# Gathering the first expert pair's tokens with the one-hot matrix as the loaded operand, and moving the first iteration's small products

## The chip, the cores and the metric

The kernel runs on one core of a Trainium2 chip. The metric is the device time of one execution in microseconds (us); lower is better. Engines are named as in the profile: PE is TensorE's matmul stream, PEld its weight loads, DVE is VectorE, ACT is ScalarE, POOL is GpSimd, SP is the engine whose queue issues the weight transfers.

## The reference, cut to what matters

One layer of a hybrid decoder: a token mixer (not touched here), LayerNorm, and then a mixture of 32 experts, of which each of the 512 tokens takes two.

```python
def _hier_moe(x, wg, bg, we, be, w1, w3, w2):
    ...
    eid = (grp[:, None] * EXPERTS_PER_GROUP + top_i).reshape(-1)      # 2 experts of each token
    ...
    xs = xpad[row_tok].reshape(n_blk, MOE_BLOCK, D)                   # the tokens of each expert
    def expert_block(args):
        xb, e = args
        h = jax.nn.silu(xb @ w1[e]) * (xb @ w3[e])
        return h @ w2[e]
    ...
    out = jnp.zeros((N + 1, D), f32).at[row_tok].add(ys * row_w[:, None])

x = _layer_norm(ALPHA * x + h, ln1_g[l], ln1_b[l])      # before the experts
x = _layer_norm(ALPHA * x + h, ln2_g[l], ln2_b[l])      # after them
```

Per expert `w1` and `w3` are 1024x512 and `w2` is 512x1024, in float32: 2 MB each.

## The kernel before

All experts are worked through in 16 pairs, `for i in range(16)`. Each expert has 64 slots, so a pair fills the 128 partitions; tokens beyond 64 for an expert go through a loop at the end (`overflow`). An iteration does, on PE: the first weights' products (`ps_a` or `ps_o <- wu,xe`, W1 then W3, each 8 contraction steps for each of the two experts, which use one half of the array's columns each), transposes of `h`, the second weights' products (W2, `ps_r` and `ps_u <- wu,hT`), and the scatter (`scatter`, `ps_w <- yh,ST` and `yl,ST`), which brings the slots' rows back to the tokens and is added into `x1` by DVE (lines 1537 to 1542). `xe` holds the pair's tokens transposed: 8 pieces of 128 features by 128 slots, feature index `8p + k`.

**Where `xe` comes from.** For pairs 1 to 15 the token rows are fetched by an indirect DMA into a tile `xg` (`gather_rows`, lines 1432 to 1441, issued by POOL, of tag `xg` with two buffers), and `turn` (lines 1515 to 1522) makes 8 PE transposes of it, in two PSUM banks, which `evacuate` copies to SBUF with LayerNorm's scale and shift, alternately on ACT and DVE. Pair 0 can't wait for a DMA: its tokens are gathered by PE. `places` (line 1383) makes a one-hot matrix `G` on DVE (128 tokens by 64 slots for each expert and each of the four token tiles `t`) from the slot numbers `posm`, which `place(t)` makes from a few small products. `gather_first(t)`, lines 1399 to 1402, then makes, for each of 8 feature groups k, one product with `x1[:, t, k::8]` as the loaded operand (128x128) and `G` as the moving one (128 columns), so that the result is already transposed. Eight pieces accumulate over the four token tiles in two PSUM banks (`w` and `o`). The last token tile's slots are known last, and two throw-away products (`NWARM`) stand in front of its gather.

**The rest of iteration 0.** Besides its own products, iteration 0 has work that the others don't: `residual(0)` and `residual(1)` (lines 1552 to 1558) scale `x1` by LayerNorm's gain and shift, spread over the partitions by 8 small products each (`row`, 16 rows of the array, `ps_w <- gb,csm`) and taken in by 8 DVE operations each; `lists` (transposes of `posm`, and counts per expert), `pair(0)` to `pair(3)` (`slot_sums`, 4 small products each, then weights and token indices), `slot_places` (the scatter's matrix `ST`) and `overflow_lists` (lines 1486 to 1506, some 20 short DVE operations, whose total `toti` is later read into a register by every engine).

**PSUM.** Small results go through tag `w`, three banks used in turn, so a product waits until the bank's former content has been read.

**Weights.** They stream through a ring of ten 2 MB buffers (`wu`), 96 units in all, issued by SP in program order. `prefetch_into(w)` reuses the buffers of W1 and W3 in quarters as soon as PE has read them (line 1111); `prefetch(2)` at the end of an iteration takes the next two buffers (line 1107), which are those of the pair's W2. The order of instructions on each engine is made by a scheduler; `tc.issue_after` fixes some of it.

Of the kernel before, what the change touches and what calls it, by code (L numbers as in the profile page):

```python
# [9 lines left out]
F32 = mybir.dt.float32  # L10
# [10 lines left out]
D = 1024  # L21
NT = S // 128
KD = D // 128
# [131 lines left out]
def trunk_kernel(ctx, tc, I, cst, out, dbg_outs=None, stop=None):  # L155
# [35 lines left out]
    def bank(tag="w"):  # L191
        return ps.tile([128, 512], F32, name="ps_" + tag, tag=tag, bufs={"w": 3, "a": 2}.get(tag, 1))
# [1201 lines left out]

    places(0, range(NT - 1))
    pk = [bank(b) for b in "wo"]
    pk = [pk[k // 4][:, 128 * (k % 4):128 * (k % 4) + 128] for k in range(KD)]

    def gather_first(t):
        for k in range(KD):  # L1400
            pe.matmul(pk[k], x1[:, t, k::KD], G_[0][:, t, 0:2].rearrange("p e s -> p (e s)").bitcast(F32),
                      start=k % 4 == 0 and t == 0, stop=k % 4 == 3 and t == NT - 1, skip_group_check=True)

    iv = place(NT - 1)
    with tc.issue_after(mm.ins):
# [10 lines left out]
    def evacuate(xe, k, p):  # L1416

        if k % 2:
            return V_.tensor_scalar(xe[:, k], p, gq[:, 0, k:k + 1], gq[:, 1, k:k + 1], op0=ALU.mult, op1=ALU.add)
        else:  # L1420
            return nc.scalar.activation(xe[:, k], p, AF.Identity, scale=gq[:, 0, k:k + 1], bias=gq[:, 1, k:k + 1])

    def xtile():
        return me.tile([128, KD, 128], F32, name="xe", tag="xe", bufs=3)
# [27 lines left out]
    def pair(i):  # L1452

        p = slot_sums(i, 0, 6)
        wv = me.tile([128, 2], F32, name="wv", tag="wv", bufs=5)
        for a in range(2):
            hp = slice(64 * a, 64 * a + 64)
            V_.tensor_copy(wv[hp, 1:2], p[hp, 2 * a + 1:2 * a + 2])
            V_.tensor_add(wv[hp, 0:1], p[hp, 2 * a:2 * a + 1], wv[hp, 1:2])
        wvs[i] = wv[:, 0:1]  # L1460
        if i > 1:
            xgs[i] = gather_rows(p[:, 4:5], 128)

    xes = {0: xtile()}
    ia = [evacuate(xes[0], k, pk[k]) for k in range(KD)][-2]
    wvs, xgs = {}, {}
    xgs[1] = gather_rows(slot_sums(1, 4, 6)[:, 0:1], 128)
    with tc.issue_after(ia.ins), tc.issue_after(iv.ins):
# [17 lines left out]
    def overflow_lists():  # L1486
        ext, one32, ends, off = (sm(n, 32) for n in ("ext", "one32", "ends", "off"))
        V_.tensor_scalar(ext, cnt, 64.0, None, op0=ALU.is_gt)
        for b in range(2, 8):
            V_.scalar_tensor_tensor(ext, cnt, 64.0 * b, ext, op0=ALU.is_gt, op1=ALU.add)  # L1490
        V_.memset(one32, 1.0)
        V_.tensor_tensor_scan(ends, one32, ext, 0.0, op0=ALU.mult, op1=ALU.add)
        toti = sm("toti", 1, dt=I32)
        V_.tensor_copy(toti, ends[:, 31:32])

        V_.tensor_sub(off, ends, ext)
        V_.tensor_scalar(off, off, -1.0, 64.0, op0=ALU.add, op1=ALU.mult)
        qo = mle
        V_.tensor_add(qo, pos, off[:, None, :].to_broadcast([128, NT, 32]))
        V_.tensor_scalar(qo, qo, 1.0, None, op0=ALU.add)  # L1500
        V_.scalar_tensor_tensor(qo, pos, 64.0, qo, op0=ALU.is_ge, op1=ALU.mult)
        qp = sm("qp", 2, NT)
        for n, o in ((0, o1), (1, o2)):
            V_.tensor_mul(wse, qo, o)
            V_.tensor_reduce(qp[:, n], wse, axis=AX.X, op=ALU.add)
        return ends, toti, qp
# [3 lines left out]
    def bk(tag):  # L1510
        t = banks[tag].pop(0)
        banks[tag].append(t)
        return bank(t)

    def turn(xg, xe, n=128):

        for h in range(2):
            p = bk("w")
            for k in range(4):
                pe.transpose(p[:, 128 * k:128 * k + n], xg[0:n, 4 * h + k::KD], ident[:n, :n])  # L1520
            for k in range(4):
                evacuate(xe, 4 * h + k, p[:, 128 * k:128 * k + n])


    HALVES = [slice(0, 512), slice(512, 1024)]
# [26 lines left out]
    def residual(n):  # L1552

        g, b = row(0, n), row(1, n)
        for t in range(NT):
            xs = x1[:, t, 512 * n:512 * n + 512]
            V_.scalar_tensor_tensor(xs, xs, ALPHA, g, op0=ALU.mult, op1=ALU.mult)
            V_.scalar_tensor_tensor(xs, b, ALPHA, xs, op0=ALU.mult, op1=ALU.add)
# [76 lines left out]
    def slot_places(es):  # L1635
        p = bk("w")
        for a in range(2):
            pe.matmul(p[64 * a:64 * a + 64], idb[0:32, es[a]:es[a] + 1].to_broadcast([32, 64]), posT[0:32], start=True, stop=True)
        ST = mh.tile([128, S], F32R, name="ST", tag="ST")
        V_.tensor_scalar(ST, p, C("slot")[:, 0:1], None, op0=ALU.is_equal)  # L1640
        return ST
# [4 lines left out]
    for i in range(16):  # L1646
        es = (2 * i, 2 * i + 1)
        xe = xes.pop(i)
        end = i == 15
        hs = []  # L1650
        for n in range(2):
            w = [units.pop((n, e)) for e in es]
            p = bk("h")
            for k in range(KD):
                for a in range(2):
                    wk = zt["half"][:, k - 4] if i + n + a == 0 and k > 3 else w[a][:, k]
                    m3 = pe.matmul(p[64 * a:64 * a + 64], xe[:, k, 64 * a:64 * a + 64], wk, start=k == 0, stop=k == KD - 1)
            hs.append(p)
            if end and not n:
                scatter(1)  # L1660
                wv, ST = wvs.pop(i), slot_places(es)
            if i > PAIRS:
                prefetch_pair() if todo else None
            elif i > FINE:
                prefetch(2)
            else:
                prefetch_into(w)
        if not i:
            hst.close()
            mh = ctx.enter_context(tc.tile_pool(name="mh", bufs=1))  # L1670
        h = mh.tile([128, 4, 128], F32, name="h", tag="h")
        nc.scalar.activation(h, fmajor(hs[0]), AF.Silu)
        V_.tensor_mul(h, h, fmajor(hs[1]))  # L1673
        if i and not end:
            with tc.issue_after(m3.ins):
                scatter(1, None, range(SC))
        elif not i:
            residual(0)
            lists()
            pair(0)  # L1680
            pair(1)
            wv, ST = wvs.pop(i), slot_places(es)
        p = bk("w")
        for f in range(4):
            pe.transpose(p[:, 128 * f:128 * f + 128], h[:, f], ident)
        hT = mh.tile([128, 4, 128], F32, name="hT", tag="h")
        nc.scalar.copy(hT, p.rearrange("p (f s) -> p f s", f=4))  # L1687
        if i and not end:
            scatter(1, None, range(SC, NT))
            wv, ST = wvs.pop(i), slot_places(es)  # L1690
        if not i:
            over = overflow_lists()
            residual(1)
        if i < 15:
            xes[i + 1] = xtile()
            turn(xgs.pop(i + 1), xes[i + 1])
        if i % 2 == 0 and i < 14:
            places(2 * i + 4, range(NT))
            pair(i + 2)
            pair(i + 3)  # L1700
        w = [units.pop((2, e)) for e in es]
        cols = PARTS if end else HALVES
        for n, cs in enumerate(cols):
            last = n == len(cols) - 1
            m = cs.stop - cs.start
            p = bk("y")[:, 0:m]
            with after(mm if n else None):
                for f in range(4):
                    for a in range(2):
                        mm = pe.matmul(p[64 * a:64 * a + 64], hT[:, f, 64 * a:64 * a + 64], w[a][:, f, cs], start=f == 0, stop=f == 3)  # L1710
            if last and end:
                overflow(*over)
            elif n and not end:
                scatter(0)
            yh = mh.tile([128, 512], F32R, name="yh", tag="yh")
            yl = mh.tile([128, 512], F32R, name="yl", tag="yl")
            nc.scalar.activation(yh[:, 0:m], p, AF.Identity, scale=wv)  # L1717
            if last and end:

                nc.scalar.activation(warm2, yh[:, 0:1].bitcast(F32), AF.Sqrt, scale=0.0, bias=epsln[:, 0:1])  # L1720
            V_.scalar_tensor_tensor(yl[:, 0:m], p, wv, yh[:, 0:m].bitcast(F32), op0=ALU.mult, op1=ALU.subtract)  # L1721
            if end and not last:
                scatter(n, add_sum, cols=PARTS)
        if i > PAIRS:
            prefetch_pair() if todo else None
        else:
            prefetch(2)
        if i == 14:

            lnq = unit([128, 2, D])  # L1730
            for n, v in enumerate(("ln2_g", "ln2_b")):
                nc.sync.dma_start(lnq[:, n], I[v][0:1].to_broadcast([128, D]))
# [64 lines left out]
```

## Time and profile before

| | before |
|---|---|
| median of 3 runs (lowest to highest) | 1120.78 us (1116.54 to 1124.68) |
| the profiled execution's own time | 1121.27 us |
| its span, first to last instruction | 1119.4 us |
| mean granted TensorE clock | 0.968 of full speed |
| PE busy | 1065.9 us, 95% |
| DVE busy | 537.7 us, 48% |
| ACT busy | 337.4 us, 30% |
| POOL busy | 267.2 us, 24% |
| HBM over the span | 237 GB/s |

The expert part begins near 598 us of the span, so the busy shares above are averages over the mixer and the experts. PE's busy time counts records whose ends are modelled: a PE that is busy all the time may still be slowed, by the clock or by its weight loads. In an f32 product two records belong to one matmul.

### The profile page before, as it was taken

How to read it: one execution, taken by the hardware profiler on the slowest of the kernel's cores; microseconds unless marked ns; L12 is line 12 of the kernel's file. 1: busy time of each engine (PE TensorE's matmuls, PEld its weight loads, DVE VectorE, ACT ScalarE, POOL GpSimd, SP SyncE). 2: the span in 40 equal slices, each digit the busy share in tenths (PEclk: the TensorE clock that was granted, in tenths of full speed). 3: DMA queues.
4: the chain of work that ended last, by engine and by line, in shares of the span. 5: the costliest groups of instructions: out<-in, count | busy, mean ns of one | idle time of the engine just before them, and what ended most of it. 6: DMA issues, size and time to landing. Idle time of an engine off the chain costs nothing. (4 is left out here: it accounts for less than half of the span.)

```text
span 1119.4 us, 16299 instructions
## 1 busy us (share of the span) xinstructions
PE 1065.9 (95%) x6172; PEld 652.7 (58%) x6172; DVE 537.7 (48%) x1382; ACT 337.4 (30%) x635; POOL 267.2 (24%) x273
## 2 busy tenths in 40 slices
PE   7999998999999999998999999999999999999992
PEld 5777766767767677786899533434343434343331
DVE  3673377468747743404555643434343434333226
ACT  4443434263463344543322211111111111111103
POOL 4541353354336245432100010101010101010003
PEclk9999898999999899999999899999999999999996
DMA  8652212302212311379847769999999999999971
GB/s 232 189 135 85 62 34 49 85 29 63 57 30 52 85 40 44 110 255 330 262 158 282 273 245 416 416 414 413 412 413 416 414 415 419 428 421 405 405 275 76
DMA packets 134896, 261.42 MB, mean 234 GB/s; under 512 B 32966, under 2 KB 89888, under 8 KB 128672
## 3 DMA queue, kind: packets, MB, share of 16 engines
q1 hardware_dynamic: 130352, 252.47, 61.2%
q0 software_dynamic: 3744, 5.73, 1.6%
q10 hardware_dynamic: 720, 2.16, 0.5%
q8 instruction: 50, 0.82, 0.3%
q14 instruction: 30, 0.25, 0.1%
HBM read 255.03 MB, written 9.72 MB: 237 GB/s over the span
## 5 line engine op out<-in xcount | busy, mean ns | idle before, releaser
L118 PE MATMUL ps_a<-wu,xe 128*64 128x512 f32 x696 | 156.5, 594 | 0.0
L118 PE MATMUL ps_w<-xh,ws 128*128 128x512 f32 (+1 forms) x432 | 150.3, 431 | 2.5 <-ACT xh L259 1.9
L118 PEld LDWEIGHTS ps_a<-wu,xe 128*64 128x64 f32 x696 | 50.0, 137 | 95.4 <-issue 90.2
L1437 POOL MEMSET xg<- 128x1024 f32 x15 | 14.2, 953 | 352.6 <-PE ps_w L122 330.0
L1540 DVE TENSOR_TENSOR x<-x,ps_w 128x512 f32<-128x512 f32 x120 | 77.0, 683 | 42.1 <-PE ps_w L118 41.0
L118 PEld LDWEIGHTS ps_w<-xh,ws 128*128 128x128 f32 (+1 forms) x432 | 79.0, 195 | 22.4 <-issue 2.2
L118 PE MATMUL ps_w<-xl,ws 128*128 128x512 f32 (+1 forms) x216 | 87.5, 411 | 0.0
L240 POOL TENSOR_TENSOR ws<-wraw,ws 128x1024 fp32r<-128x1024 f32 (+2 forms) x31 | 67.4, 2175 | 76.8 <-ACT ws L239 76.6
L118 PE MATMUL ps_r<-wu,hT 128*64 128x512 f32 (+1 forms) x272 | 81.2, 611 | 0.7 <-ACT hT L1687 0.7
L118 PE MATMUL ps_w<-xh,w 128*128 128x512 f32 x224 | 76.0, 416 | 0.0
L118 PE MATMUL ps_o<-wu,xe 128*64 128x512 f32 x320 | 71.9, 594 | 0.0
L118 PE MATMUL ps_u<-wu,hT 128*64 128x512 f32 (+1 forms) x256 | 70.4, 581 | 0.0
L1673 DVE TENSOR_TENSOR h<-h,ps_a 128x512 f32<-128x512 f32 x11 | 7.6, 688 | 126.5 <-PE ps_a L118 126.5
L118 PE MATMUL ps_w<-yh,ST 128*128 128x512 f32 (+1 forms) x132 | 58.4, 453 | 4.4 <-ACT yh L1717 3.0
L884 POOL TENSOR_SCALAR pt<-pt,sm,gs 128x128 f32<-128x128 f32 (+3 forms) x64 | 44.6, 703 | 68.6 <-DVE sm L882 45.4
L239 ACT CAST ws<-wraw 128x1024 fp32r<-128x1024 f32 (+2 forms) x43 | 39.6, 922 | 45.8 <-DMA wraw<-in_w_up_rwkv_dram 9.9
L881 ACT ACTIVATE pt<-pt,sm 128x128 f32<-128x128 f32 (+3 forms) x64 | 35.5, 556 | 57.4 <-DVE sm L879 56.9
L118 PEld LDWEIGHTS ps_w<-yh,ST 128*128 128x128 f32 x132 | 24.3, 188 | 47.2 <-issue 23.1
L118 PE MATMUL ps_w<-yl,ST 128*128 128x512 f32 (+1 forms) x132 | 50.3, 393 | 0.3 <-DVE yl L1721 0.3
L118 PEld LDWEIGHTS ps_o<-wu,xe 128*64 128x64 f32 x320 | 22.6, 137 | 44.4 <-issue 43.6
L118 PEld LDWEIGHTS ps_w<-xl,ws 128*128 128x128 f32 (+1 forms) x216 | 41.7, 193 | 10.9 <-issue 0.9
L1687 ACT COPY hT<-ps_w 128x512 f32<-128x512 f32 x16 | 9.4, 586 | 122.7 <-PE ps_w L122 122.7
(463 smaller groups left out, 1945.1 us busy)
## 6 DMA issues: line engine op xcount, KB each, us to landing
wu<-in_exp_w_dram SPq DMA_DIRECT2D x198, 512.0 KB, 10.2
wu<-in_exp_w_dram SPq DMA_DIRECT2D x35, 2048.0 KB, 16.5
wu<-in_exp_w_dram SPq DMA_DIRECT2D x20, 1024.0 KB, 19.3
wraw<-in_w_in_dram SPq DMA_DIRECT2D x36, 512.0 KB, 3.9
wraw<-in_w_out_dram SPq DMA_DIRECT2D x8, 512.0 KB, 5.4
rrep<-rrow_d SPq DMA_DIRECT2D x4, 640.0 KB, 7.8
xin<-in_x_dram SPq DMA_DIRECT2D x4, 512.0 KB, 5.5
wraw<-in_w_in_dram SPq DMA_DIRECT2D x8, 256.0 KB, 3.7
```

The costliest lines, as they stand in the source:

```text
L118: return self.e.matmul(out, lhsT, rhs, **kw)
L239: hi_eng(hi[:, :w], raw[:, :w])
L240: (eng or nc.gpsimd).tensor_sub(lo[:, :w], raw[:, :w], hi[:, :w].bitcast(F32))
L881: nc.scalar.activation(pt[:, :n], pt[:, :n], AF.Exp, scale=-1.0, bias=sm[:, 0:1], accum_out=sm[:, 1:2])
L884: nc.gpsimd.tensor_scalar(pt[:, :n], pt[:, :n], sm[:, 1:2], gs[:, i, gi:gi + 1], op0=ALU.mult, op1=ALU.mult)
L1437: nc.gpsimd.memset(xg[0:n], 0.0)
L1540: V_.tensor_add(x1[:, t, cols[n]], x1[:, t, cols[n]], p)
L1673: V_.tensor_mul(h, h, fmajor(hs[1]))
L1687: nc.scalar.copy(hT, p.rearrange("p (f s) -> p f s", f=4))
```

## The change

It has three parts. (1) `gather_first` loads `G` (128 tokens by 128 slots) and moves the rows of `x1`, 512 columns at a time, so two products per token tile stand for eight; the result is the pair's token rows, not transposed. ACT and DVE copy the two banks into a tile `xg`, and `turn`, now defined earlier, transposes it like the other pairs' rows. (2) `residual(0)` is called behind the W1 products instead of behind the multiplication of `h`. (3) `slot_places(0)` comes behind the transposes of `h`, and `overflow_lists` goes from iteration 0 to iteration 1.

```diff
     pk = [bank(b) for b in "wo"]
-    pk = [pk[k // 4][:, 128 * (k % 4):128 * (k % 4) + 128] for k in range(KD)]
     def gather_first(t):
-        for k in range(KD):
-            pe.matmul(pk[k], x1[:, t, k::KD], G_[0][:, t, 0:2].rearrange("p e s -> p (e s)").bitcast(F32),
-                      start=k % 4 == 0 and t == 0, stop=k % 4 == 3 and t == NT - 1, skip_group_check=True)
+        for n in range(2):
+            pe.matmul(pk[n], G_[0][:, t, 0:2].rearrange("p e s -> p (e s)").bitcast(F32), x1[:, t, 512 * n:512 * n + 512],
+                      start=t == 0, stop=t == NT - 1)
...
+    def turn(xg, xe, n=128):
+        last = None
+        for h in range(2):
+            p = bank()
+            for k in range(4):
+                pe.transpose(p[:, 128 * k:128 * k + n], xg[0:n, 4 * h + k::KD], ident[:n, :n])
+            for k in range(4):
+                e = evacuate(xe, 4 * h + k, p[:, 128 * k:128 * k + n])
+                last = last if k % 2 else e
+        return last
...
-    ia = [evacuate(xes[0], k, pk[k]) for k in range(KD)][-2]
+    xg = me.tile([128, D], F32, name="xg", tag="xg", bufs=2)
+    nc.scalar.copy(xg[:, 0:512], pk[0])
+    V_.tensor_copy(xg[:, 512:1024], pk[1])
+    ia = turn(xg, xes[0])
...
             hs.append(p)
+            if not i and not n:
+                residual(0)
...
         elif not i:
-            residual(0)
             lists()
             pair(0)
             pair(1)
-            wv, ST = wvs.pop(i), slot_places(es)
...
         if not i:
-            over = overflow_lists()
+            wv, ST = wvs.pop(i), slot_places(es)
             residual(1)
...
+        if i == 1:
+            over = overflow_lists()
```

What the scheduler makes of it shows in the instruction order. First PE in the middle of the gather (`trib` and `oneb` belong to `place`, `ps_u <- selb` are its products, `x_4920` is `x1`, `ps_a <- x_4920` are the throw-away products):

```order
-L118 MATMUL ps_w<-G,x_4920 128x128 x3
-L118 MATMUL ps_o<-G,x_4920 128x128 x4
-L118 MATMUL ps_w<-G,x_4920 128x128 x4
-L118 MATMUL ps_o<-G,x_4920 128x128 x2
+L118 MATMUL ps_o<-x_4920,G 128x512
+L118 MATMUL ps_w<-x_4920,G 128x512
+L118 MATMUL ps_o<-x_4920,G 128x512
 L118 LDWEIGHTS trib
 L118 MATMUL ps_u<-selb,trib 128x32
-L118 MATMUL ps_o<-G,x_4920 128x128 x2
-L118 MATMUL ps_a<-x_4920 128x256
+L118 MATMUL ps_a<-x_4920 128x256 x2
```

The placing product of token tile 2 stood behind 14 gather products of tiles 0 and 1 (one of them above these rows) and now stands behind all four long ones; both throw-away products moved in front of the gather of tile 2.

PE around the end of iteration 0's W1 products, where `ps_w <- gb` are the row products of `residual(0)` and `posm` the transposes of `lists`:

```order
 L118 MATMUL ps_a<-half,xe 64x512
-L118 MATMUL ps_a<-wu,xe 64x512 x17
+L118 MATMUL ps_a<-wu,xe 64x512
 L118 MATMUL ps_w<-gb_5481,csm 128x128 x8
+L118 MATMUL ps_a<-wu,xe 64x512 x16
 L122 MATMUL ps_w<-csm,posm 32x128 x4
```

The 8 row products went from behind the 16 W3 products to the place ahead of them; the DVE operations that read them go ahead of the multiplication of `h` in the same way.

SP's queue around the 14 loads into the quarters of iteration 0's W1 and W3 buffers (line 1111) and the two whole loads into its W2 buffers (line 1107), before and then with the change:

```order
L1107 DMA wu<-in_exp_w_dram 128x4096 x3
L1111 DMA wu<-in_exp_w_dram 128x1024 x14
L1566 TENSOR_LOAD toti
L1566 ISA x2
L1107 DMA wu<-in_exp_w_dram 128x4096 x2
```

```order
L1111 DMA wu<-in_exp_w_dram 128x1024 x4
L1107 DMA wu<-in_exp_w_dram 128x4096 x3
L1111 DMA wu<-in_exp_w_dram 128x1024 x14
L1107 DMA wu<-in_exp_w_dram 128x4096 x2
L1111 DMA wu<-in_exp_w_dram 128x1024 x16
```

The read of `toti` leaves this place and now stands behind the last weight loads and the loads of the last LayerNorm's parameters.

## Rows read from the trace of the kernel before

**Rows 1.** Busy time by stretch: engines' busy us (instructions), granted clock, DMA share, GB/s.
```profile
628.90:642.40 13.50, 11.17 (x60) 9.28 (x58) 11.66 (x36) 1.16 (x2) 0.00 (x0) 0.68 0.65 259
637.40:653.40 16.00, 16.00 (x61) 7.92 (x60) 10.53 (x35) 2.99 (x6) 0.95 (x1) 0.69 0.02 7
653.40:1086.00 432.60, 429.17 (x1914) 168.81 (x1916) 159.20 (x343) 63.02 (x115) 25.32 (x26) 1.00 1.01 408
```

**Rows 2.** Timeline of ACT: start us, duration, instruction, [idle before <- releaser]; W1's evacuations.
```profile
664.35 0.60 ACT L1672 ACTIVATE h<-ps_o 128x512 f32<-128x512 f32 x1 [5.63 <-PE ps_o L118]
692.85 0.60 ACT L1672 ACTIVATE h<-ps_a 128x512 f32<-128x512 f32 x1 [6.60 <-PE ps_a L118]
...
1040.72 0.60 ACT L1672 ACTIVATE h<-ps_a 128x512 f32<-128x512 f32 x1 [6.60 <-PE ps_a L118]
```

**Rows 3.** Timeline of PE, first pair's gather and its first W1 products.
```profile
597.95 0.72 PE L118 MATMUL ps_w<-G,x 128*128 128x128 f32 x2
...
610.40 0.60 PE L118 MATMUL ps_a<-x 128*128 128x256 f32 x2
610.84 1.96 PE L118 MATMUL ps_w<-G,x 128*128 128x128 f32 x8
...
614.99 1.51 PE L118 MATMUL ps_a<-wu,xe 128*64 128x512 f32 x6
```

**Rows 4.** Timeline of DVE in the gather.
```profile
601.80 0.19 DVE L1307 TENSOR_TENSOR selb<-o,o 128x32 bf16<-128x32 f32 x1
...
605.07 0.19 DVE L1314 SCALAR_TENSOR_TENSOR posm<-ps_u,selb 128x32 f32<-128x32 f32 x1 [2.70 <-PE ps_u L118]
...
605.30 0.43 DVE L1389 TENSOR_TENSOR G<-posm,csm 128x256 fp32r<-128x256 f32 x1
...
606.42 0.19 DVE L1307 TENSOR_TENSOR selb<-o,o 128x32 bf16<-128x32 f32 x1
```

**Rows 5.** Busy time by stretch, the two in which the granted clock was down.
```profile
599.60:603.10 3.50, 3.50 (x16) 3.50 (x16) 2.67 (x15) 0.00 (x0) 1.22 (x2) 0.51 1.00 387
...
633.80:647.40 13.60, 13.35 (x46) 8.38 (x48) 12.05 (x42) 1.04 (x2) 0.00 (x0) 0.50 0.28 110
```

**Rows 6.** Timeline of PE from the end of W3's products in iteration 0.
```profile
628.88 2.04 PE L118 MATMUL ps_w<-gb,csm 16*128 16x128 f32 x16
...
633.80 1.02 PE L118 MATMUL ps_w<-wsp,G 128*128 128x6 f32 x4 [1.42 <-DVE x L1557]
...
637.69 3.77 PE L118 MATMUL ps_w<-gb,csm 16*128 16x128 f32 x16
...
642.45 6.11 PE L118 MATMUL ps_r<-wu,hT 128*64 128x512 f32 x16
...
654.31 0.59 PE L118 MATMUL ps_u<-wu,hT 128*64 128x512 f32 x1
```

**Rows 7.** Timeline of DVE in the same stretch, `residual(0)` and the copy behind it.
```profile
630.07 1.28 DVE L1557 SCALAR_TENSOR_TENSOR x<-x,ps_w 128x512 f32<-128x512 f32 x2 [0.30 <-PE ps_w L118]
...
634.86 0.18 DVE L1483 COPY cnt<-ps_w 128x32 f32<-128x32 f32 x1
```

**Rows 8.** Groups by line: a DVE copy of a whole bank, elsewhere: busy us, mean ns.
```profile
L903 DVE COPY tp<-ps_w 128x512 f32<-128x512 f32 x8 | 5.5, 689 | 2.5 <-PE ps_w L122 2.4
```

**Rows 9.** Timeline of iteration 1, a bank's copy by ACT, and `turn` with its evacuations.
```profile
672.78 0.59 ACT L1687 COPY hT<-ps_w 128x512 f32<-128x512 f32 x1 [7.83 <-PE ps_w L122]
...
675.41 1.16 PE L122 MATMUL ps_w<-csm,xg 128*128 128x128 f32 x8
676.17 1.84 ACT L1421 ACTIVATE xe<-ps_w,gq 128x128 f32<-128x128 f32 x4 [2.80 <-PE ps_w L122]
```

**Rows 10.** SP queue's waits, 610 to 670 us: us in total, times, longest.
```profile
SPq L1566 <- DVE toti L1494: 12.1, 1, 12.1
SPq L1107 <- PE ps_u L118: 10.1, 1, 10.1
```

**Rows 11.** Timeline of PE, the last pair's W2 products.
```profile
1084.10 3.65 PE L118 MATMUL ps_r<-wu,hT 128*64 128x512 f32 x16 [0.68 <-ACT hT L1687]
```

More of the change, by code (lines that the diff above doesn't have):

```diff
@@ L1513, in bk @@
         return bank(t)
[L1515 to L1522, printed above, removed]
     HALVES = [slice(0, 512), slice(512, 1024)]
```

## The prediction

> **What bounds the kernel now.** I read the stretch table first, then the timelines of PE, DVE and ACT from 595 to 665 us, then SP's waits. From iteration 1 on PE sets the pace: W1's result is taken up by ACT at 664.35 us, then 28.5 us later, and the last of 13 further times at 1040.72, in steps of 28.5 and 29.5 us that repeat to the hundredth [rows 2]; from 653.4 to 1086 us PE is busy for 429.17 of 432.6 us at the full clock [rows 1]. The weights' transfers run at 408 GB/s over the same stretch, a DMA share of 1.01: they are full too. PE is only just served. The last pair's W2 products begin at 1084.10 us [rows 11], about when the stream ends. So what is saved before 653 us counts only if PE and the transfers both come earlier.
>
> They do hang on one place. Between 637.4 and 653.4 us the transfers stand still (DMA share 0.02) [rows 1]: the ring is full, and SP waits 10.1 us for the end of iteration 0's W2 products on `ps_u` before it issues the next two units [rows 10]. Whatever brings that end (654.31 + 0.44 = 654.75 us) [rows 6] earlier moves the full stream and PE's steady part alike, and the end of the kernel with them, 1:1. The sum is therefore made at this end. It has three stretches: the gather up to the first W1 product, 597.95 to 614.99 us [rows 3]; W1 and W3, 614.99 to 628.88, 13.89 us at the full clock [rows 3, 6]; and the rest up to 654.75, 25.87 us, of which 13.6 us have a granted clock of 0.50 [rows 5], that is the 1.2 GHz level.
>
> **Part 1, the gather.** *Removed:* 8 products per token tile. In the last tile 4 of them take 1.80 us (610.84 to 612.64, the eight records of that row are four matmuls), the tile's eight some 3.6 us. *Added:* 2 products of 512 columns. No such f32 product over the whole array stands in the trace; the nearest is the throw-away product of 256 columns, whose follower starts 0.44 us later (610.40 to 610.84) [rows 3], so 0.88 us for 512 columns and 1.76 us for a tile. That is the full clock; at the lower level double.
>
> The gather is not a plain sum of products, since `place` of tiles 2 and 3 stands in PE's queue between them. Tile 2's `selb` is made by 602.0 us, but DVE waits 2.70 us until PE, behind 14 slow products, has made the placing product, and starts `posm` at 605.07; the rest of tile 3's routing stands behind `posm` on DVE [rows 4]. With the change, PE does tiles 0 and 1 in 4 x 0.88 + 0.3 (two placing products in between) = 3.8 us, to 601.8, and is then ready as `selb` comes. So `posm` at 602.3, `G` of tile 2 by 603.1 (0.8 us as in [rows 4], one short operation now ahead of it), tile 3's `selb` at 603.6 (1.3 us from the start of `G` to the end of `selb` in [rows 4], less that operation). PE meanwhile does the throw-away products (0.88) and tile 2; tile 3's `G` is there at 605.3, and its two products run to 607.1.
>
> Then come the new costs, which nothing hides, because PE has only this to do: a copy of each bank, on ACT 0.59 [rows 9] and on DVE 0.69 us [rows 8]. The ACT copy runs under the last product, so 0.75 us with the hand-over. The 8 transposes take 1.16 us, and the first evacuations start 0.76 us after the transposes do [rows 9], under the rest of them and under the 4 slot sums (0.5 us). First W1 product: 607.1 + 0.75 + 1.16 + 0.55 = **609.55 us, 5.4 us earlier.** The bounds: the clock was down from 599.6 to 603.1 [rows 5], which the old products did not feel (1.8 to 2.0 us per eight records at either level), but which would cost the new ones some 1.3 us: then 610.8. It fell after a second in which PE had waited for routing; the new products fill the time before the fall better, so I take the value without. The worst is rival A.
>
> **Part 2, `residual(0)` ahead of W3.** Its 8 products cost PE 2.04 us wherever they stand [rows 6]. The 8 DVE operations, 630.07 to 634.86 us, 4.8 us [rows 7], now lie beside W3's 6.95 us and are over about 2 us before it ends, so a ready DVE takes up the multiplication of `h` at once. W3 ends at 609.55 + 13.89 + 2.04 = 625.5 us.
>
> Behind W3, before: 13.57 us to the first W2 product (628.88 to 642.45), of which 2.04 were the rows, about 3 us waiting (for a free bank, the longest 1.42, on `residual(0)`), and from 633.80 on 8.65 us of products at the lower clock: sums 1.02, row products 3.77 [rows 6]. With the change the waits on `residual(0)` go, and the same products stay: 8.65 / 2 = 4.3 us at the full clock, 0.9 for the transposes and counts ahead of them, and 1.0 for banks that DVE has still to read (it makes the pair weights, two `G` and `ST` there). Together 6.2 us at the full clock.
>
> **Part 3, the order behind W3.** `slot_places` behind the transposes of `h` takes `ST` off the way to `hT`. `overflow_lists`, some 20 operations of 0.14 to 0.3 us on DVE, goes to iteration 1 under 14 us of W1 and W3 products, where DVE has the time (159.20 busy of 432.6 us) [rows 1]: nothing. On SP the read of `toti` held the queue for 12.1 us, but the 10.1 us wait for `ps_u` followed [rows 10], so taking it away alone is worth nothing; left in place it could have become the limit. At its new place SP has issued every load.
>
> **The clock behind W3 is the open size.** In rows: it fell at 633.8 us, 4.9 us after the dense W3 products ended, and rose at 647.4, 5.0 us after the dense W2 products began [rows 5, 6]. With the same two delays here: W3 ends at 625.5, the fall comes when 1.3 of the 6.2 us are still to do, they take 2.6, and W2 begins 7.5 us behind W3, at 633.0. W2 with what is put between its products needs 6.95 + 0.55 (second half of `turn`) + 1.0 (pair sums) = 8.5 us at the full clock. 5.0 us at the lower level do 2.5 of them, the other 6.0 run at the full one: end at **644.0 us.** Without any fall: 625.5 + 6.2 + 8.5 = 640.2.
>
> **Sum.** 654.75 - 644.0 = 10.8 us: 5.4 from the gather, 13.57 - 2.04 - 7.5 = 4.0 behind W3, and 12.3 - 11.0 = 1.3 in W2. The scatter behind it is the same work. Against the profiled execution: 1121.27 - 10.8 = 1110.5 us. The median of the runs is 0.5 us lower (1120.78), so I say **1110 us**. Own range of this case: 1107.5 to 1112.5.
>
> **Rivals.**
>
> *A, the gather's new pause costs the clock.* Between the last gather product and the first W1 product PE now has 0.75 us of nothing and 1.7 us of short products. A fall there would put 3.5 us or more of W1 at the lower level: +1.7 to +2.5 us, and with the earlier fall (1.3) up to 3.8. For it: both falls here came after sparse seconds [rows 5, 6]. Against it: the pause is half as long as the sparse stretch behind W3. Time: 1110 + 3 = 1113 us. The Trainium skill, "TensorE: Matmul & The Clock Gate", section "HAM oscillation — how this bites in real kernels", says that bursts of matmuls parted by waits let the clock fall, and that each next burst starts slow; it speaks against putting a copy between gather and weights. The trace agrees that sparse stretches end at the lower level, behind W3; whether this pause is sparse enough no row shows.
>
> *B, the clock does not fall behind W3,* since the stretch is now half as long: 654.75 - 640.2 = 14.5 us, 1106 us. Against it: over 4.9 us of sparse work remain, as many as before the fall in the rows.
>
> *C, the gain stops at the transfers.* PE runs 11 us earlier, but the stream, full from 653.4 us on, arrives only as much earlier as it starts. It starts at the end of W2, so it gains the same; C holds only if something else than W2's end holds the restart (SP queue order, a quarter load late). Then 1117 to 1121 us. The 10.1 us wait speaks against it [rows 10].
>
> *D, slower: the low clock of A does not end.* If PE stayed at 1.2 GHz through all of W1 and W3, these would take 13.9 us more, and the end of W2 would come at 644 + 13.9 = 658 us, 3 us later than now: 1124 us. It decides where more than 11 us of dense products run at the lower level. Against it: the clock rose 5.0 us after dense work began [rows 5, 6].
>
> *E, the moves bring nothing by themselves* (bank waits take the place of those removed): the gather's 5.4 us alone, 1115.5 us.
>
> **How the numbers follow.** Main case 0.50, A 0.18, B 0.13, C 0.06, D 0.05, E 0.08. Range for 8 in 10: from B's side 1105 to E's side 1117. About 1% (11.2 us) is what a measurement of this kernel can tell from no change; the runs of before lie 8 us apart. The main case sits at 0.96% and is split: some 0.25 of its 0.50 fall below 1109.6 us. With B, and a little of A, faster by over 1%: 0.40. Slower by over 1% needs 1132 us, more than D gives, and stands for what I have not seen: 0.04. The rest, 0.56, lies within 1%.
>
> **What would show it.** The profile after: eight gather records of 512 columns at about 0.44 us apart, and the first W1 product near 609.5 us (right for part 1; over 611, A or the earlier fall). `x` operations of `residual(0)` under W3, and no wait on them behind it (part 2). First W2 product 6 to 8 us behind W3, and W2's end 10 to 11 us earlier, with the idle stretch of the transfers shorter by about as much less the gather's share. Iterations of 28.5 and 29.5 us as now. Wrong would be: a wait on `xg` of over 2 us, a clock that falls under W1, or a stream that restarts later than W2 ends.

## The result, and the profile after

Over 20 runs each the changed kernel takes 1115.82 us (median, 1109.13 to 1123.67) and the kernel before 1120.93. The ratio is 0.9947, 95% interval 0.9923 to 0.997: 5.9 us faster, with 2.6 us to either side, so faster, but within 1%. Forecast were 1110 us in 1105 to 1117, 10.8 us less. The profiled execution took 1115.31 us, a span of 1113.5 us.

The stretches of the changed kernel's trace, one for each stage of the prediction (busy us of PE, weight loads, DVE, ACT, POOL, then granted clock, DMA share, GB/s); from above: the gather, W1 and W3, the stretch from W3's end to the end of W2, the steady part, and what follows from the last pair's W2 products on:

```profile
599.70:612.20 12.50, 11.67 (x42) 5.75 (x41) 7.13 (x44) 2.89 (x6) 1.11 (x2) 0.86 1.00 409
612.20:628.20 16.00, 16.00 (x81) 6.27 (x80) 9.99 (x42) 5.90 (x18) 1.93 (x2) 1.00 0.95 364
628.20:646.10 17.90, 16.91 (x89) 8.58 (x87) 13.83 (x47) 3.46 (x7) 0.95 (x2) 0.90 0.44 172
646.10:1076.00 429.90, 426.52 (x1898) 167.57 (x1898) 159.38 (x343) 62.99 (x115) 25.56 (x26) 1.00 1.01 409
1076.00:1113.50 37.50, 16.18 (x72) 8.02 (x72) 19.81 (x44) 12.76 (x21) 8.59 (x4) 0.71 0.22 86
```

W1 and W3 run wholly at the full clock, as before; the two stretches that the change is about have a granted clock of 0.86 and 0.90. The steady part is what it was: DMA share 1.01, 409 GB/s [rows 1].

The timeline of PE in the same trace, the ends of the stages (start us, duration, instruction, count):

```profile
599.70 1.76 PE L118 MATMUL ps_w<-x,G 128*128 128x512 f32 x2
...
608.94 1.02 PE L118 MATMUL ps_o<-x,G 128*128 128x512 f32 x2
610.79 1.14 PE L122 MATMUL ps_w<-csm,xg 128*128 128x128 f32 x8 [0.83 <-issue]
...
612.20 3.65 PE L118 MATMUL ps_a<-wu,xe 128*64 128x512 f32 x16
...
628.21 0.61 PE L122 MATMUL ps_w<-csm,posm 128*32 128x128 f32 x4
...
634.48 5.16 PE L118 MATMUL ps_r<-wu,hT 128*64 128x512 f32 x14
...
644.16 1.93 PE L118 MATMUL ps_u<-wu,hT 128*64 128x512 f32 x6
```

Counted from the first gather product, as the prediction does, the first W1 product comes at 12.5 us (before 17.04 [rows 3]), the first W2 product at 34.8 (44.5 [rows 6]) and the end of W2, 644.16 + 1.93 = 646.09, at 46.4. In before that end is 56.8 by the prediction's mark, and 56.96 with the last record's whole 0.59 us, which the table further down uses for all kernels. So at the end of W2 the gain is 10.4 to 10.6 us, where 10.8 was forecast. Only some 6 us reach the end of the kernel, and the rest is in three places.

**Ahead of the gather.** The first gather product starts at 599.70 us in this execution and at 597.95 in that of before, though nothing in front of it was changed. The clock fell there once more, at 535.2 us, for 3.4 us. Half of that, 1.7 us, is the difference: chance of one execution.

**Between the end of W2 and iteration 1.** From the end of W2 to the point where ACT takes up W1's result of iteration 1 pass 10.30 us, 9.45 in before [rows 2]. In before one product of the next pair's W1 runs beside W2's last one [rows 6], each in one half of the array's columns; in the changed kernel it comes behind. The two records of that product in before:

```profile
653.84 0.64 PE L118 MATMUL ps_o<-wu,xe 128*64 128x512 f32 x1
...
654.32 0.59 PE L118 MATMUL ps_o<-wu,xe 128*64 128x512 f32 x1
```

So 0.85 of the 10.6 us is only the place of the mark, and 9.7 us arrive at the steady loop.

**Behind the last W2 products.** From their first to the end of the span pass 37.46 us (1076.08 to 1113.5), 35.3 in before [rows 11]. Nobody touched that code. The timeline of ACT there, first of before, then of the changed kernel:

```profile
1098.87 1.28 ACT L1720 ACT_TABLE_LOAD   x1
...
1101.84 1.15 ACT L1746 ACTIVATE sq<-x,nmu 128x1024 f32<-128x1024 f32 x1 [1.38 <-DVE nmu L1744]
...
1103.11 0.29 ACT L1744 ACTIVATE lsd<-lsd,epsln 128x1 f32<-128x1 f32 x1
```

```profile
1090.21 1.28 ACT L1727 ACT_TABLE_LOAD   x1
...
1093.41 1.28 ACT L1753 ACT_TABLE_LOAD   x1 [1.62 <-PE ps_w L118]
1094.71 1.15 ACT L1753 ACTIVATE sq<-x,nmu 128x1024 f32<-128x1024 f32 x1
...
1095.97 1.28 ACT L1751 ACT_TABLE_LOAD   x1
1097.27 0.29 ACT L1751 ACTIVATE lsd<-lsd,epsln 128x1 f32<-128x1 f32 x1
```

In before one table load stands ahead of the LayerNorm's squares `sq` and roots `lsd`, in a place where ACT waits anyway; the first root starts 1.27 us behind the first square. In the changed kernel two more loads stand in this chain. One is between the first square and the first root, which makes that step 2.56 us; the other, ahead of the square, is mostly hidden, since ACT would wait there for DVE's `nmu` in any case. DVE's first reciprocal, and with it the whole end, waits for that root.

The order of instructions on ACT says why. Of before:

```
L1566 TENSOR_LOAD toti
L1569 COMPARE_AND_BRANCH
...
L1717 ACTIVATE yh<-ps_r,wv 128x256
L1720 ACT_TABLE_LOAD
L1720 ACTIVATE warm_5531<-yh,epsln 128x1
L1746 ACTIVATE sq,lsd<-x_4920,nmu 128x1024
L1744 ACTIVATE lsd<-lsd,epsln 128x1
```

And of the changed kernel:

```
L1724 ACTIVATE yh<-ps_r,wv 128x256
L1727 ACT_TABLE_LOAD
L1727 ACTIVATE warm_5531<-yh,epsln 128x1
L1571 TENSOR_LOAD toti
L1574 COMPARE_AND_BRANCH
...
L1753 ACT_TABLE_LOAD
L1753 ACTIVATE sq,lsd<-x_4920,nmu 128x1024
L1751 ACT_TABLE_LOAD
L1751 ACTIVATE lsd<-lsd,epsln 128x1
```

The last `yh` and the early root `warm`, whose only purpose is to fetch the table in good time, have moved ahead of the overflow loop (`toti` and the branch). The loop's body, which does not run here, now has table loads of its own in the built program, and what was loaded ahead of it doesn't count behind it. Behind the loop the first function decides: where a root comes first, as in before, one load serves the roots and the squares between them; where a square comes first, it gets one load and the root behind it another. The Trainium skill, "ScalarE activation tables: per-element evaluation and per-set limits", section "Table sets in the compiler and the runtime", says of the compiler's back end that it places table loads per block, by the longest run of functions that a set serves. No run here tests that rule, since these loads stand in the built program already; the two loads for one square and one root are not what it would give.

### The profile page after: what moved, and what is told of

Its sections match the earlier page's. It is cut to its first block, busy times and chain, and to the rows that moved or that the text cites. A ratio compares the mean times of both kernels' runs of the same rounds, so it can differ in the third digit from the quotient of the medians.

```text
span 1113.5 us, 16225 instructions
## 1 busy us (share of the span) xinstructions
PE 1059.4 (95%) x6132; PEld 640.1 (57%) x6132; DVE 538.6 (48%) x1383; ACT 340.5 (31%) x638; POOL 268.2 (24%) x273
## 3 DMA queue, kind: packets, MB, share of 16 engines
q10 hardware_dynamic: 720, 2.16, 0.5%
HBM read 255.03 MB, written 9.72 MB: 238 GB/s over the span
## 5 line engine op out<-in xcount | busy, mean ns | idle before, releaser
L239 ACT CAST ws<-wraw 128x1024 fp32r<-128x1024 f32 (+2 forms) x43 | 39.6, 921 | 44.7 <-DMA wraw<-in_w_up_rwkv_dram 10.2
L118 PEld LDWEIGHTS ps_w<-xl,ws 128*128 128x128 f32 (+1 forms) x216 | 41.5, 192 | 10.9 <-issue 0.9
## 6 DMA issues: line engine op xcount, KB each, us to landing
wu<-in_exp_w_dram SPq DMA_DIRECT2D x198, 512.0 KB, 10.2
```

What stands on the lines that cost most here:

```text
L118: return self.e.matmul(out, lhsT, rhs, **kw)
L239: hi_eng(hi[:, :w], raw[:, :w])
```

## The experiments

All times below are from profiles, counted from the first gather product, since what lies in front of it is the same in all and differs by up to 11 us with the clock. "h of iteration 1" is where the steady loop is met (the ACT evacuation of W1); "end" is from the first product of the last W2 to the end of the span. "Clock down" is where in the gather or behind W3 it was, and for how long. r0, l0, s0 and l1 were executed once each, so they are read by their stages alone; every other ratio is to the kernel before on the same chip.

| kernel | first W1 | W3's end | first W2 | end of W2 | h of iter. 1 | end | total | clock down |
|---|---|---|---|---|---|---|---|---|
| before | 17.04 | 30.99 | 44.49 | 56.96 | 66.41 | 35.30 | 521.45 | gather 3.4, W2 13.7 |
| changed | 12.49 | 28.57 | 34.77 | 46.39 | 56.69 | 37.46 | 513.84 | gather 3.4, W2 3.4 |
| after2 (changed again) | 10.90 | 26.98 | 33.05 | 44.82 | 55.12 | 37.47 | 512.37 | W2 3.4 |
| g1 (gather alone) | 10.90 | 24.85 | 38.34 | 50.80 | 60.25 | 35.27 | 515.30 | W2 13.7 |
| gold (moves alone) | 17.11 | 33.19 | 40.84 | 52.55 | 62.85 | 37.47 | 520.17 | gather 3.4, W2 6.8 |
| r0 | 10.90 | 24.85 | 38.33 | 49.46 | 59.76 | 37.46 | 516.99 | W2 10.2 |
| l0 | 10.90 | 26.98 | 35.06 | 45.73 | 57.05 | 37.45 | 514.20 | W2 6.8 |
| s0 | 10.90 | 26.98 | 33.11 | 44.89 | 54.16 | 37.46 | 511.95 | W2 3.4 |
| l1 (lists' move alone) | 17.05 | 31.00 | 44.73 | 55.92 | 65.19 | 37.47 | 522.97 | W2 10.2 |
| tail | 10.90 | 26.98 | 33.05 | 44.84 | 55.14 | 35.83 | 510.70 | W2 3.4 |
| hold | 12.49 | 28.57 | 35.02 | 46.38 | 56.68 | 35.83 | 512.21 | gather 3.4, W2 3.4 |
| rows1 | 10.90 | 26.98 | 31.60 | 42.81 | 53.50 | 35.84 | 508.96 | none |

Between h of iteration 1 and the last W2 lie 419.6 to 420.3 us in every kernel.

**after2: the changed kernel once more.**

> The changed kernel again, unchanged, on the chip of the next three. Theory T (stages): from the first gather product to the end of iteration 0's W2 products 46.4 us (before 56.8), from the first product of the last W2 to the end of the span 37.4 us (before 35.3), whatever the clock did ahead of the gather; 1110 to 1118 us. Rival L (luck): the 37.4 us behind the last W2 are the clock's doing in that one execution, and come out nearer 35.3 here.

Ratio to before 0.9942 (0.9909 to 0.9975), as in the first comparison. The end takes 37.47 us again: not luck. Nor is it the clock, which falls in every end: 17.3 us behind the first product of the last W2 in before, 15.4 in the changed kernel, but 18.3 in r0, and r0's end takes 37.46 us all the same. The gather is 1.6 us shorter than expected, since the clock did not fall in it this time. The stretches of the gather and of the fall behind W3:

```profile
605.50:616.40 10.90, 10.07 (x41) 5.26 (x40) 7.05 (x44) 2.83 (x6) 1.07 (x2) 1.00 1.00 404
...
638.60:642.10 3.50, 3.50 (x11) 1.07 (x12) 3.50 (x7) 0.46 (x1) 0.00 (x0) 0.52 0.47 183
```

**g1: the new gather alone.** The kernel before with `gather_first`, the copies to `xg` and the `turn` of the first pair as changed.

> The kernel before with part 1 alone (the new gather). Theory T: first W1 product 12.5 us behind the first gather product instead of 17.0; the end of iteration 0's W2 products 4.5 us earlier (52.3 us behind the first gather product) unless the clock falls elsewhere behind W3; the end as before with one table load on ACT, 35.3 us; 1116 to 1117 us. Rival C (the gain stops at the transfers): the first W1 product comes 4.5 us earlier, the end does not, 1121 us.

Ratio 0.9957 (0.9925 to 0.9988), some 4.8 us faster. The first W1 product comes 6.15 us earlier and not 4.5, since the clock did not fall in this gather. The PE timeline:

```profile
599.52 1.10 PE L118 MATMUL ps_w<-x,G 128*128 128x512 f32 x2
...
607.15 1.02 PE L118 MATMUL ps_o<-x,G 128*128 128x512 f32 x2
609.01 1.13 PE L122 MATMUL ps_w<-csm,xg 128*128 128x128 f32 x8 [0.83 <-issue]
...
610.41 1.94 PE L118 MATMUL ps_a<-wu,xe 128*64 128x512 f32 x8
```

The 6.15 us by which the first W1 product comes earlier are 6.16 at the end of W2, 6.16 in the steady loop, and 6.15 in the total. The end is that of before, with one table load. That is the 1:1 rule of the prediction, seen undisturbed; rival C falls.

**gold: the moves alone.** The changed kernel with the old `gather_first` and its evacuations.

> The changed kernel with the old gather, so parts 2 and 3 alone. Theory T: first W1 product 17.0 us behind the first gather product, the end of W2 50.9 us behind it (5.9 earlier than before), but the end carries the two further table loads on ACT, 37.4 us instead of 35.3; together 1117 us. Rival E (the moves bring nothing by themselves): end of W2 about 55 us behind the gather's start, 1121 to 1123 us.

Ratio 0.9985 (0.9955 to 1.0014): no difference can be measured. The end of W2 comes 4.4 us earlier, not 5.9, since here the clock was down for 6.8 us behind W3 and not 3.4. From there to h of iteration 1 pass 10.30 us and not 9.45: as in the changed kernel, 0.85 of the 4.4 are only the place of the mark. The end costs 2.17 more: 521.45 - 520.17 = 1.3 us are left. Rival E gets the measured time, but for another reason than its own: the moves do gain 3.6 us up to h of iteration 1, and give 2.2 back behind the last W2.

**l1: the move of `overflow_lists` alone, in the kernel before.**

```diff
         if not i:
-            over = overflow_lists()
             residual(1)
...
+        if i == 1:
+            over = overflow_lists()
```

> The kernel before with `overflow_lists` moved to iteration 1 and nothing else. In the built program this alone puts `yh` and the square root of ACT ahead of the overflow loop, with two further table loads behind it. Theory T: the first product of the last W2 to the end of the span takes 37.4 us instead of 35.3, although the moved work itself lies 450 us earlier; the gather as before (17.0 us to the first W1 product). Rival: the 2.1 us come with the new gather or `residual(0)`, and 35.3 stays.

The end takes 37.47 us, and ACT shows the same three table loads:

```profile
1101.07 1.28 ACT L1721 ACT_TABLE_LOAD   x1
...
1104.28 1.28 ACT L1747 ACT_TABLE_LOAD   x1 [1.62 <-PE ps_w L118]
...
1106.84 1.28 ACT L1745 ACT_TABLE_LOAD   x1
```

Moved 450 us ahead of it, some 20 short operations on DVE change the order of the end. But they are not the only cause: in l0 (below), which has them back in iteration 0 and the other moves in place, the end still takes 37.45 us. In the built programs the move of `residual(0)` alone does the same, and the gather or `slot_places` alone does not. What in the scheduler decides it is left open.

**tail: the end mended.** The early root reads a value that the overflow loop writes (`cur`), so that it must stand behind the loop.

```diff
+        return cur
...
-                overflow(*over)
+                past = overflow(*over)
...
-                nc.scalar.activation(warm2, yh[:, 0:1].bitcast(F32), AF.Sqrt, scale=0.0, bias=epsln[:, 0:1])
+                nc.scalar.activation(warm2, past, AF.Sqrt, scale=0.0, bias=epsln[:, 0:1])
```

> The changed kernel, with the early square root that loads ACT's table made to read a value written inside the overflow loop, so that it stands behind that loop on ACT; the result of it is not used either way. Theory T: one table load behind the loop in place of two beside one ahead of it; the first `lsd` comes about 1.7 us earlier, and the first product of the last W2 to the end takes 35.7 us instead of 37.4; 1.7 us under the changed kernel. Rival L: the table loads lie in the shadow of something else, and 37.4 stays.

```profile
1086.46 1.28 ACT L1728 ACT_TABLE_LOAD   x1 [2.19 <-DVEq L1574]
...
1088.43 1.15 ACT L1754 ACTIVATE sq<-x,nmu 128x1024 f32<-128x1024 f32 x1 [0.39 <-DVE nmu L1752]
...
1089.70 0.29 ACT L1752 ACTIVATE lsd<-lsd,epsln 128x1 f32<-128x1 f32 x1
```

One load, and ACT waits 0.39 us behind it: the root is 1.27 us behind the square, as in before. The end takes 35.83 us (35.7 expected), 1.64 less. Ratio to before 0.993 (0.99 to 0.996), which after2's interval overlaps: the 1.64 us are read from the stage, and hold and rows1 (below), with the same mend, show 35.83 and 35.84. So of the 2.16 us, 1.64 are the table loads. The last 0.5 remain ahead of them: `yh` and `yl` still stand ahead of the loop, and DVE leaves the loop's branch 17.3 us behind the first product of the last W2, 15.8 in before, so that its first `nmu` comes 0.55 later.

**r0: `residual(0)` back behind W3, all else changed.**

> The changed kernel with `residual(0)` back behind W3. By the prediction's part 2: W1 and W3 take 2.1 us less (14.0), and the stretch from W3's end to the first W2 product more than 2.04 longer than 6.1 us, since its 4.8 us on DVE stand ahead of the pair weights again: 10 to 12 us; from the first gather product to the end of W2 2 to 4 us more than 44.8. Rival E: the rows' 2.04 us only change place, 8.1 us behind W3 and 44.8 in all.

W1 and W3 take 13.95 us, as expected, but W2 starts 13.48 us behind W3, more than the 10 to 12 expected, and the end of W2 comes 4.6 us later than in after2, not 2 to 4. The PE timeline behind W3:

```profile
629.32 2.05 PE L118 MATMUL ps_w<-gb,csm 16*128 16x128 f32 x16
...
634.25 0.61 PE L118 MATMUL ps_w<-wsp,G 128*128 128x6 f32 x4 [1.42 <-DVE x L1562]
635.45 1.01 PE L118 MATMUL ps_w<-wsp,G 128*128 128x6 f32 x4 [0.59 <-DVE x L1563]
...
638.11 3.78 PE L118 MATMUL ps_w<-gb,csm 16*128 16x128 f32 x16
```

The wait of 1.42 us on `residual(0)` is back [rows 6], and behind it the lower clock, at which the second rows take 3.78 us and not 2.02. The clock is most of it: 10.2 us at the lower level against 3.4 in after2 cost half of 6.8, 3.4 of the 4.6 us. And it is no single execution: with `residual(0)` behind W3 the clock was down for 10.2 to 13.7 us in all four profiles (before, g1, l1, r0), with it under W3 for 6.8 at most in all eight others. This one call carries nearly all that the moves gain.

**l0 and s0: `overflow_lists` and `slot_places` back, one at a time.**

> The changed kernel with `overflow_lists` back in iteration 0 (ahead of `residual(1)`). By the prediction's part 3 its 20 short operations on DVE cost nothing in iteration 1, so what they cost in iteration 0 is the gain of the move: from W3's end to the first W2 product 6.1 us if none of them is waited for, up to 10 us if all of them (about 4 us on DVE) stand ahead of a bank that PE wants. I expect 6.1 to 7. SP's read of `toti` in iteration 0 either holds the two units' loads behind the end of W2 (then the stream restarts over 1 us after it) or not.

> The changed kernel with `slot_places` back ahead of the transposes of `h`. By the prediction's part 3 its move takes `ST` (0.75 us on DVE) off the way to `hT`: then W3's end to the first W2 product takes up to 0.8 us more than 6.1 here; if PE has other work there, 6.1 stays. I expect 6.1 to 6.5, and the end as in the changed kernel (37.4 us).

In l0 the first W2 product comes 8.08 us behind W3 (6.1 to 7 expected) and h of iteration 1 comes 1.9 us later. None of it is waiting: PE waits once, 0.80 us (0.98 in two waits in after2), but the second rows ran at the lower clock.

```profile
636.17 3.75 PE L118 MATMUL ps_w<-gb,csm 16*128 16x128 f32 x16 [0.80 <-DVE wv L1458]
```

The fall came 3.3 us behind W3 in this execution and 6.0 in after2, and the clock was down for 3.4 us more, which is 1.7 of the 1.9; whether the move brought that on, one execution can't say. SP restarts the stream at 650.29 us, 1.3 us ahead of the end of W2, so `toti` does not hold it. In s0 the stretch is 6.13 us and the total 0.4 us below after2's: the move of `slot_places` brings nothing here.

**hold: a throw-away product against the fall of the clock**, on top of tail, behind the transposes of `h`.

```diff
-            pe.transpose(p[:, 128 * f:128 * f + 128], h[:, f], ident)
+            tr = pe.transpose(p[:, 128 * f:128 * f + 128], h[:, f], ident)
+        if not i:
+            with tc.issue_after(tr.ins):
+                pe.matmul(bank("o"), ident, xgs[1][:, 0:512], start=True, stop=True)
```

> The kernel with the mended end and one throw-away product of 512 columns (0.94 us at the full clock) behind the transposes of `h`, where PE waits 0.28 and 0.70 us. If the sparse stretch is what lets the clock fall, there is no fall behind W3, W2 takes about 10.1 us instead of 11.8, and its end comes 1.3 to 1.7 us earlier (43.1 to 43.5 us behind the first gather product). Rival: one product more does not keep the clock, and the end of W2 comes 0 to 0.9 us later (44.8 to 45.7).

```profile
631.86 1.02 PE L118 MATMUL ps_o<-xg,csm 128*128 128x512 f32 x2
...
633.41 2.02 PE L118 MATMUL ps_w<-gb,csm 16*128 16x128 f32 x16 [0.19 <-DVE wv L1458]
...
635.50:638.90 3.40, 3.40 (x10) 1.30 (x12) 3.40 (x7) 0.46 (x1) 0.00 (x0) 0.50 0.68 269
```

The product fills the two waits (0.98 us of waiting become 0.19), and the clock falls all the same, 5.6 us behind W3. The rival was right: the end of W2 lies 46.38 us behind the gather's start, 44.79 without the 1.59 that the fall in this execution's gather cost. The ratio is 0.9917 (0.9883 to 0.995), which tail's interval overlaps.

**rows1: the sparse stretch made shorter**, on top of tail: `residual(1)` behind the first half of W2 instead of ahead of it.

```diff
             wv, ST = wvs.pop(i), slot_places(es)
-            residual(1)
...
+            if not i and not n:
+                residual(1)
```

> The kernel with the mended end, and `residual(1)` put behind the first 16 products of W2 instead of ahead of them. If the sparse stretch behind W3 is what costs the clock and the waits, it shrinks from 6.1 to about 4.1 us, and the end of W2 comes 0.7 us earlier (the wait for the pair weights goes) with a fall of the clock as now, or 2.4 us earlier without one: 44.1 or 42.4 us behind the first gather product in place of 44.8. Rival: the work is only moved, and DVE, with 4.8 us more during W2, becomes late for the copies of `xe` and `yl`: 44.8 or more.

```profile
626.20:630.90 4.70, 3.76 (x35) 3.19 (x33) 4.09 (x16) 1.62 (x4) 0.00 (x0) 1.00 1.02 408
630.90:642.10 11.20, 11.20 (x56) 4.94 (x55) 10.08 (x36) 1.99 (x4) 2.98 (x3) 1.00 0.42 150
```

W2 begins 4.62 us behind W3, the granted clock is 1.00 through all of it, and the end of W2 comes 2.0 us before tail's (2.4 expected), h of iteration 1 1.6 us. Ratio to before 0.9904 (0.9869 to 0.9939), 10.8 us: by its total (508.96 us) 1.7 us below tail and 3.4 below the changed kernel with the same gather (after2). Its interval overlaps tail's and hold's, and 1.7 of the 2.0 us are the missing fall (half of 3.4), in one execution: that the shorter stretch keeps the clock is suggested, not shown.

## Why the prediction held, and which step did not

**The 1:1 rule.** From the restart of the stream to the last pair all went as said. In the changed kernel SP waits 15.7 us for `ps_u`, 10.1 in before [rows 10], with the read of `toti` gone from the queue:

```profile
SPq L1107 <- PE ps_u L118: 16.2, 2, 15.7
```

The stream restarts at 645.28 us, 0.8 us ahead of the end of W2 and, counted from the first gather product, 9.9 us earlier than in before (653.40), and the steady loop is unchanged: from h of iteration 1 to that of the last pair pass 410.69 us, 410.74 before [rows 2]. What fails is "and the end of the kernel with them, 1:1". The sum stopped at the end of W2, on the word that all behind it is the same work. It is the same work, but not the same order: 2.16 us of the forecast gain went into the end, 1.64 of them, by l1 and tail, through the place of one table load. This could have been read before any run, since the order of the changed kernel's instructions shows two table loads behind the loop and one ahead of it, where before has one behind it. The prediction looked only at the order in the places that the diff names.

**The gather.** 11.6 us were forecast at the full clock, 12.85 with the fall; 10.90 and 12.49 were measured. The product of 512 columns starts its follower after 0.86 to 0.94 us (0.88 forecast); tile 3's last products end 8.67 us behind the start, not 9.15; the copies leave PE 0.83 us idle (0.75), the transposes take 0.89 (1.16), the slot sums 0.52 (0.55). The choice that the clock would not fall there was right in seven of the nine profiles with the new gather, and wrong in the one that was compared.

**W1, W3 and the rows**: 15.93 forecast, 16.08 measured, full clock throughout: rivals A and D did not come.

**Behind W3**: 7.5 forecast, 6.20 measured, which is the 6.2 given for the full clock. The work was sized rightly; the fall came 5.9 us behind W3 instead of 4.9, when it was nearly over. **W2**: 11.0 forecast, 11.61 measured. Of the low stretch 3.1 us lay in W2 and not 5.0, which saves 1.0; but the products with what stands between them need 11.61 - 1.5 = 10.1 us at the full clock, not 8.5. The term was undersized by 1.6. In part that is one turn more: the 16 products run two at a time, one in each half of the columns, which makes 8 turns in 6.95 us, but with other products between them it takes 9, since a group of 7 (the 14 records at 634.48) and one of 3 (the 6 at 644.16) each leave one without a partner. The misses in the gather (0.9 with the fall), behind W3 (1.3 the other way) and in W2 (0.6) nearly cancel, and that is luck. Rival B (no fall) came only in rows1.

**Part 3** was taken at nothing. `slot_places` is nothing (s0). `overflow_lists` gains up to 1.9 us where it was (l0, mostly the clock) and costs 2.2 at the end when it is moved alone (l1); in the changed kernel taking that move back does not mend the end (l0). Rival E's 1115.5 us is nearest to the measured time, but its reason is wrong: `residual(0)` alone is worth 4.6 us at the end of W2 (r0).

**The sum.** For the two profiled executions, from the table: 9.72 us gained up to h of iteration 1, 2.16 lost at the end, 1.75 by the clock in front of the gather, 0.05 in the loop: 5.9 of span. The forecast time was too low by 5.8 us. Its range held, but the narrower one of its main case, 1107.5 to 1112.5, did not: that case had the end of W2 and the loop right, but not the 0.85 us between them and the 2.16 us at the end of the kernel.

## What to carry over

A gain ahead of the steady part does pass through 1:1 when PE and the transfers restart together, but a scheduler may pay for it elsewhere: compare the order of every engine to the last row, table loads above all, even where the diff says nothing. An instruction that is there only to fetch something early needs a dependency that holds its place; here one operand brought back 1.6 us. Where a stretch of short products costs the clock, filling its waits did not help, and making it shorter did, in one execution of each.

## What was not expected of the hardware

**The old gather does not feel the clock, the new one does.** The old one takes 17.04 and 17.11 us to the first W1 product with 3.4 us at the lower level, and 17.05 in l1, whole at the full one:

```profile
601.00:618.50 17.50, 17.50 (x86) 17.28 (x85) 7.65 (x45) 2.35 (x6) 1.88 (x2) 1.00 0.92 375
```

There PE's weight loads are busy 17.28 of 17.5 us. In before a load of the old gather takes 0.34 us and the next product record starts 0.24 us behind the last, at the lower level (600.36 to 602.75 us) as at the full one (610.97 to 614.32 us), so I read the loads as its pace. The new one, with 5.26 of 10.90, takes 10.90 or 12.49.

**The spread of the runs is mostly the clock.** The shortest of the changed kernel's 20 runs (1109.13 us) has a mean granted clock of 0.978, the longest (1123.67) 0.963. In the profiles, the first gather product comes between 595.28 us (27.3 us at the lower level before it, tail) and 606.17 us (48.0, gold). Taking away half of the time at the lower level leaves 579.2 to 582.2 us for all twelve, 3.0 us of the 10.9. A change of a few us is therefore read from stages counted from a common mark, not from one time.
